# Half-product pairs that begin one pair later and leave one ordinary pair between them, with other banks before them and another order at the end

## The chip, the cores and the metric

The kernel runs on one core of one Trainium2 chip. The metric is the device time of one execution in microseconds (us). Five engines work side by side and wait for each other through semaphores: TensorE (PE) multiplies matrices, VectorE (DVE), ScalarE (ACT) and GpSimd (POOL) work on elements, and SyncE (SP) issues most of the DMAs. Results of PE stand in banks of PSUM; DVE and ACT read them there and so set the bank free for a later matmul.

## The reference

One decoder layer on 512 tokens of width 1024 in float32. A token-mixing part (two causal mixers, their projections, a residual) takes the first two thirds of the time and is not touched here. The channel-mixing part follows:

```python
h = rms_norm(x, norm_ffn_pre[l])
u = causal_dwconv(h @ ffn_up[l], ffn_conv_w[l], ffn_conv_b[l])
u_gate, u_val = jnp.split(u, 2, axis=-1)
x = x + rms_norm((jax.nn.silu(u_gate) * u_val) @ ffn_down[l], norm_ffn_post[l])
```

`ffn_up` has 2 x 2816 columns, that is 44 blocks of 128, or 22 pairs of a gate block and a value block; the convolution has width 3 along the tokens.

## The kernel before, in words

**Numbers in two parts.** Every operand of a matmul is split into a high part (a copy by ACT in a rounded format, L134 or L1698) and a low part (what the rounding lost, a subtraction on DVE or POOL, L172 or L1699). A product is made of three matmuls: high by high, high by low, low by high. So each weight tile of 128x512 costs one DMA, one copy on ACT (the "high", a tile name that ends in h) and one subtraction (the "low", a name that ends in l).

**The up projection** goes over pairs j = 0 to 21. Blocks 2j and 2j + 1 are the pair's gate and value. There are three ways to compute a pair:

- *Ordinary pairs*, those before the first half-product pair, run two blocks of 24 matmuls over 512 tokens (`mm3`). Their weights go through `split_w` with tiles of the pool wp: three buffers for highs and lows (WB), four for raw tiles (RAWB). All their lows are on POOL. The result of block b stands in one of the banks pj, px, py, pz in turn (two buffers each). The name is up with the block and the half: up110 and up111 are block 11's two tiles, pu its result.
- *Half-product pairs* (`seven`, the pairs listed in SEVEN) save one product in eight: with sums and differences of weights and of token quarters, seven products of twelve matmuls over 256 tokens take the place of eight. The results g, v and t stand in PSUM as sg, sv and st; t is always in pz, g and v both in pj for odd pairs, and in px and py for even ones. DVE combines them (L1578). The weights are called sw with the pair and a number: 5, 2, 1, 3, 6, 4, 8 in the order in which PE uses them. Of the seven lows five are on POOL, those of 1 and 8 on DVE. The token forms tf0 to tf3, which these products need, are made by DVE and ACT beside the ordinary pairs.
- *Ordinary pairs between them* (`plain`, L1605) run the same matmuls as the first kind, by quarters, with four sw weights.

The sw weights come from a generator (`coming`), and each product calls the next one, so that five are always ahead. `form_w` deals them out to two rings of buffers by their running number: three of eight go to wp, where the ordinary pairs have theirs as well, five of eight to a ring of their own, sw.

**Eviction of a block.** ACT scales it with the middle tap of the convolution (L1643), DVE adds the two other taps (L1644, L1645), and only then is the bank free. Then come SiLU on ACT (L1653 or L1657) and the product of gate and value (L1654 for ordinary pairs, on POOL, and on DVE for the last two; L1659 for the others), a difference for pairs under 11 (L1661), and the high and the low of the result (L1662, L1667) for the down projection.

**Beside it** POOL issues DMAs that add up weights in DRAM, first for half-product pairs (fs), then for the down projection (ds). The generator `ws` issues one of them at fixed places: one or two for a pair.

**The down projection** uses the same trick: seven products dn of a 2x2 split, each over eleven weight tiles dw and two token tiles. `down_w` takes them in the order of a running number n, loads them and splits them; the low is on POOL when n % 3 is 1. The last product (m = 6) stops four weights short, and these four, the tail (n = 73 to 76), are run token tile by token tile. The sums of the products for the token tiles 2 and 3 are complete when product 5 ends. `post` then does the last step for a token tile: the sum of squares (ACT, L1394), a product with the norm's gain (tm, L1397), the inverse root (ACT, then a reciprocal on DVE, L191), two scalings with the residual added (L1401) and a store of each half. It is called for tiles 2 and 3, and, after the tail's matmuls, for tiles 0 and 1.

**What sets the order.** Each engine runs its instructions in the order of its own queue. A scheduler makes these orders from the program's order and its own estimates; `keep` and `late` hold an instruction to the program's order. Where two engines need a tile they wait for each other by semaphores.

Of the kernel before, what the change touches and what calls it, by code (L numbers as in the profile page):

```python
# [10 lines left out]
F32 = mybir.dt.float32  # L11
F32R = mybir.dt.float32r
AF = mybir.ActivationFunctionType
OP = mybir.AluOpType
# [5 lines left out]
D = 1024  # L20
# [5 lines left out]
V_GMIX, V_GFFN, V_MU, V_MUL, V_W0, V_A0, V_KK, V_KA, V_RK, V_LNW, V_LNB = 0, 8, 16, 40, 43, 51, 59, 67, 75, 83, 91  # L26
WB = 3
RAWB = 4
SEVEN = (6, 7, 8, 9, 10, 11, 12, 14, 15, 16, 18, 19, 20, 21)
SGRP = 2  # L30
UPOS = {j: i for i, j in enumerate(SEVEN + tuple(sorted(set(range(22)) - set(SEVEN))))}
RB = 4
KH, TL = 11, 4
# [19 lines left out]
def hybrid_layer(ctx: ExitStack, tc: tile.TileContext, a, out, dbg=None, stop=None):  # L53
    nc = tc.nc
    te, ve, sc, po, sy = nc.tensor, nc.vector, nc.scalar, nc.gpsimd, nc.sync
# [9 lines left out]
    wp = pool("wp", c=ctx)  # L65
# [43 lines left out]
    junk = xp.tile([128, 1], F32, name="junk")  # L109
# [78 lines left out]
    def rstd_of(ss, n, name, p):  # L188
        st = p.tile([128, 2], F32, tag=name[:2] + "st", name=name, bufs=4)
        act(st[:, 0:1], ss, AF.Sqrt, bias=eps6, scale=1.0 / n)  # L190
        ve.reciprocal(st[:, 1:2], st[:, 0:1])  # L191
        return st[:, 1:2]
# [208 lines left out]
    p2 = lp[2]  # L401
# [572 lines left out]
    for g in range(2):  # L974
        group_tiles(g)
        for i in range(GP):
            p = GP * g + i
# [414 lines left out]
    def post(acc, res, ss, gb, name, p, t, each, x2):  # L1392
        junk = p.tile([128, 512], F32, tag=name + "jk", name=f"{name}jl{t}", bufs=1)
        sc.activation(junk, acc, AF.Square, accum_out=ss[:, 1:2])  # L1394
        tm = p.tile([128, 512], F32, tag=name + "tm", name=f"{name}tm{t}", bufs=2)
        ve.tensor_tensor(ss[:, 2:3], ss[:, 0:1], ss[:, 1:2], op=OP.add)
        ve.tensor_tensor(tm, acc, gb[:, 512:], op=OP.mult)  # L1397
        r = rstd_of(ss[:, 2:3], D, f"{name}r{t}", p)
        for i, q in enumerate((res[:, t, :], tm)):
            hs = slice(i * 512, i * 512 + 512)  # L1400
            ve.scalar_tensor_tensor(x2[t][:, hs], q, r, x2[t][:, hs], op0=OP.mult, op1=OP.add)  # L1401
            each(t, hs)

    op = pool("op", "left", octx)
    x2 = op.tile([128, 4, D], F32, name="x2")
# [74 lines left out]
    with pool("ff") as ff:  # L1480
# [55 lines left out]
        keep = tc.keep_in_program_order  # L1536
        ring = itertools.count()

        def form_w(src, name, eng):
            n = next(ring)  # L1540
            p_, tags, b = (wp, ("raw", "whi", "wlo"), (RAWB, WB)) if n % 8 % 3 == 1 else (sw, ("sraw", "shi", "slo"), (4, 5))
            hi = p_.tile([128, 512], F32R, tag=tags[1], name=name + "h", bufs=b[1])
            lo = p_.tile([128, 512], F32R, tag=tags[2], name=name + "l", bufs=b[1])
            split_to(src, hi, lo, name, 512, eng, p_, late=n < 5, tag=tags[0], bufs=b[0])
            return hi, lo
# [71 lines left out]
        for j in range(22):  # L1617
            us = []
            sv_ = None
            if j == 2:  # L1620
                sw = pool("sw", "right", sctx2)
            if j == SEVEN[0]:
                for _ in side:
                    pass
            if j >= SEVEN[0]:
                sv_ = (seven if j in SEVEN else plain)(j)
            for x in range(2):
                blk = 2 * j + x
                if blk < NU:
                    p = pu4[blk]  # L1630
                    half_up(blk, 1)
                elif sv_ is not None:
                    p = sv_[x]
                else:
                    wh, wl = after.get(blk) or split_w(upw(blk), f"up{blk}")
                    p = ((pj, px, py, pz)[blk % 4] if j < SEVEN[0] else pj)(f"pu{blk}")
                    mm3(p, wslice(wh), wslice(wl), lambda k: h2h[:, k, :], lambda k: h2l[:, k, :])
                if blk == 2 * SEVEN[0] - 1:
                    for _ in range(5):
                        next(coming)  # L1640
                cv = blk * 4
                u = fu.tile([128, S], F32, tag=f"u{x}", name=f"u{blk}", bufs=2)
                sc.activation(u, p, AF.Identity, scale=cvec[:, cv + 2:cv + 3], bias=cvec[:, cv + 3:cv + 4])  # L1643
                ve.scalar_tensor_tensor(u[:, 1:], p[:, :S - 1], cvec[:, cv + 1:cv + 2], u[:, 1:], op0=OP.mult, op1=OP.add)  # L1644
                ve.scalar_tensor_tensor(u[:, 2:], p[:, :S - 2], cvec[:, cv:cv + 1], u[:, 2:], op0=OP.mult, op1=OP.add)  # L1645
                us.append(u)
                if j < SEVEN[0]:
                    for _ in range(1):
                        next(side, None)
                if (j > 2 or x == 0 if j < SEVEN[0] else x == 0 or j not in SEVEN):  # L1650
                    next(ws, None)
            if sv_ is None:
                sc.activation(us[0], us[0], AF.Silu)  # L1653
                (ve if j > SEVEN[0] - 3 else po).tensor_tensor(us[1], us[0], us[1], op=OP.mult)  # L1654
                y = us[1]
            else:
                sc.activation(sv_[0], us[0], AF.Silu)  # L1657
                y = sv_[1] if j >= KH else us[1]
                ve.tensor_tensor(y, us[1], sv_[0], op=OP.mult)  # L1659
            if j < KH:  # L1660
                ve.tensor_tensor(y[:, rgt], y[:, rgt], y[:, lft], op=OP.subtract)  # L1661
            high = sc.activation(ah[:, j, :], y, AF.Copy)  # L1662
            if j == 20:
                last[high.ins.engine] = high
            if j < KH:
                tc.keep_in_program_order(sc.dma_start(t1d[j], y[:, rgt]))
            ve.tensor_tensor(al[:, j, :], y, ah[:, j, :].bitcast(F32), op=OP.subtract)  # L1667
            if j >= KH:
                if j == KH:
                    t2ctx = ExitStack()  # L1670
                    t2 = pool("t2", "left", t2ctx)
                    t1s = [t1_load(0), t1_load(1)]
                else:
                    sy.dma_start(t24d[j - 1 - KH], t24)
                t24 = t2.tile([128, S], F32, tag="t24", name=f"t24{j}", bufs=2)
                ve.tensor_tensor(t24[:, lft], y[:, rgt], t1s[j - KH], op=OP.subtract)
                if j < 20:
                    t1s.append(t1_load(j - KH + 2))
                ve.tensor_tensor(t24[:, rgt], y[:, lft], t24[:, lft], op=OP.subtract)
            if j == 1:  # L1680
                f4ctx.close()
# [3 lines left out]
        def down_w(f, k):  # L1685
            n = next(ring)
            src = a["down4"][f[0], f[1], k] if isinstance(f, tuple) else dsum[k // 2][f][k % 2]
            if n < WB:
                hi, lo = (wp.tile([128, 512], F32R, tag=t, name=f"dw{t}{n}", bufs=WB) for t in ("whi", "wlo"))
            else:  # L1690
                hi, lo = (y[:, (n - WB) % 8, :] for y in (h2h, h2l))
            if n < 8 or n > 9 and n % 8 < 2 or n % 8 >= 6:
                raw = wp.tile([128, 512], F32, tag="raw", name=f"dw{n}r", bufs=RAWB)
            elif n < 10:
                raw = sw.tile([128, 512], F32, tag="sraw", name=f"dw{n}r", bufs=4)
            else:
                raw = ep.tile([128, 512], F32, tag="draw", name=f"dw{n}r", bufs=4)
            load, high = sy.dma_start(raw, src), sc.activation(hi, raw, AF.Copy)  # L1698
            low = (po if n % 3 == 1 else ve).tensor_tensor(lo, raw, hi.bitcast(F32), op=OP.subtract)  # L1699
            if WB <= n < 10:  # L1700
                behind(high)
            if n >= 10:
                keep(load)
                keep(high)
                keep(low)
            return hi, lo
# [5 lines left out]
        with pool("ep") as ep:  # L1712
            res2 = ep.tile([128, 4, 512], F32, name="res2")
            pa, u4 = ([ep.tile([128, 512], F32, name=f"{n}{i}") for i in range(2)] for n in ("pa", "uf"))
            t24 = ep.tile([128, KH, S], F32, name="t24")
            g3 = ep.tile([128, D], F32, name="gb4")
            ep.tile([128, 512], F32, tag="p2jk", name="p2jk", bufs=1)
            s2, x2 = {}, {}

            def store(t, hs):  # L1720
                sy.dma_start(out[t * 128:(t + 1) * 128, hs], x2[t][:, hs])
# [76 lines left out]
            def add(o, x, y, op=OP.add):  # L1798
                return ve.tensor_tensor(o, x, y, op=op)
# [33 lines left out]
            p2 = down(1, (0, 1), 1, 0, py, copies(p1))  # L1833
            p5 = down(2, 0, 0, 1, pz, first_half(p2))
            p4 = down(3, 3, 1, 1, pj, squares(p2), 0)
            p = down(4, 1, 0, 1, px)
            load_x2(0)
            p7 = down(5, 2, 0, 0, py, second_half(p, p5, p4))
            p = down(6, (1, 1), 1, 0, px)
            tail = [down_w((1, 1), k) for k in range(KH - TL, KH)]  # L1840
            for i in range(2):
                keep(add(pa[i], p7[i], pa[i]))
                keep(add(p7[i], p7[i], u4[i]))
                post(p7[i], res2, s2[2 + i], g3, "p2", ep, 2 + i, store, x2)
            for i in range(2):
                for k in range(KH - TL, KH):
                    mms(p[i], 1, 0, k, i, tail[k - KH + TL], False, k == KH - 1)
# [104 lines left out]
```

## Time and profile before

| What | Value |
|---|---|
| three runs, median (lowest to highest) | 1149.72 us (1146.75 to 1150.6) |
| the profiled execution | 1141.52 us, span 1139.7 us |
| PE busy | 1108.8 us, 97% of the span |
| DVE, ACT, POOL busy | 760.7, 644.2, 607.4 us |
| PE's longest wait from 770 us to the end | 6.5 us, at 859 us |
| granted TensorE clock, mean | 0.994 |

Times in rows are us from the start of the span. A row of a timeline has the start, the duration, the engine, the line of the kernel, the operation, output<-inputs, shapes, and, in brackets, how long the engine had stood idle before it and what ended that. PE's matmuls overlap, so their cadence is read from the starts. A row of the waits has who waited for whom: the sum, how often, the longest.

### The profile page before, as it was taken

The numbers are of one execution on the slowest core, as the hardware profiler recorded it, in microseconds if no ns is written. First come the engines' busy times: TensorE is split into PE (matmuls) and PEld (weight loads), VectorE is DVE, ScalarE is ACT, GpSimd is POOL, SyncE is SP. The second block draws the span as 40 slices with busy tenths as digits, with TensorE's granted clock in tenths as the row PEclk, the third lists the DMA queues.
The fourth block names the chain that finished last, engine by engine and source line by source line (L and its number), as shares of the span: only waits on it lengthen the run. The fifth ranks groups of instructions, "written<-read, shape, count | busy, mean of one in ns | idle before, by whom it ended". The sixth has DMA issues, their size and how long they took to land.

```text
span 1139.7 us, 21485 instructions
## 1 busy us (share of the span) xinstructions
PE 1108.8 (97%) x7776; PEld 911.7 (80%) x7776; DVE 760.7 (67%) x1443; ACT 644.2 (57%) x1266; POOL 607.4 (53%) x617
## 2 busy tenths in 40 slices
PE   9999999999999999999999999999997999999996
PEld 7888888877888887767667778888887999897885
DVE  4236655735665553697787745754897987887897
ACT  6447763544666334486666653543555665665554
POOL 4346765545766454576555534540567675654431
PEclk9999999999999999999999999999998999999998
DMA  7524568543666896327576546685677788879983
GB/s 273 133 71 123 153 168 223 158 121 88 184 144 173 236 259 206 94 85 183 175 222 170 133 144 197 204 267 162 193 190 200 248 265 235 268 251 327 292 280 117
DMA packets 121676, 217.00 MB, mean 190 GB/s; under 512 B 37601, under 2 KB 43297, under 8 KB 114914
## 3 DMA queue, kind: packets, MB, share of 16 engines
q1 hardware_dynamic: 95986, 147.07, 40.9%
q0 software_dynamic: 8144, 52.70, 19.7%
q10 hardware_dynamic: 17440, 15.86, 4.4%
q8 instruction: 61, 1.00, 0.3%
q14 instruction: 45, 0.37, 0.1%
HBM read 186.81 MB, written 77.99 MB: 232 GB/s over the span
## 4 chain that ended last, share of the span: by engine, by line
PE 79%; DVE 9%; DMA 5%; ACT 3%; issue 2%; POOL 2%; SPq 0%; ACTq 0%; DVEq 0%; POOLq 0%
PE sg L1573 4%; PE st L1573 4%; PE gt L349 3%; PE ub L1277 3%; PE gt L351 3%; PE gt L350 3%; PE pt L150 3%; PE o L1219 2%; PE ub L1279 2%; PE ub L1278 2%; PE v L349 2%; PE v L350 2%; PE v L351 2%; PE dn L1779 2%; PE dn L1780 2%
## 5 line engine op out<-in xcount | busy, mean ns | idle before, releaser
L1167 ACT ACTIVATE p<-p,stt 128x384 f32<-128x384 f32 (+3 forms) x128 | 70.6, 554 | 31.1 <-DVE stt L1165 30.5
L1165 DVE CUSTOM_DVE_ANT_0 p<-s,rh 128x384 f32<-128x384 f32 (+3 forms) x128 | 59.2, 484 | 20.2 <-PE s L1151 17.1
L1139 POOL TENSOR_SCALAR p<-p,stt 128x512 f32<-128x512 f32 (+1 forms) x64 | 38.8, 613 | 40.8 <-DVE stt L1132 26.3
L1780 PE MATMUL dn<-hh,al 128*128 128x512 f32 x148 | 57.6, 389 | 0.0
L1779 PE MATMUL dn<-hl,ah 128*128 128x512 f32 x148 | 57.6, 389 | 0.0
L1778 PE MATMUL dn<-hh,ah 128*128 128x512 f32 x148 | 57.1, 389 | 0.0
L150 PE MATMUL pt<-ident,p 128*128 128x128 f32 x320 | 44.5, 273 | 1.3 <-DVE p L1141 1.2
L1158 PE MATMUL s<-kst,qs 128*128 128x512 f32 (+1 forms) x128 | 39.1, 395 | 5.8 <-DVE stt L1165 5.6
L150 PEld LDWEIGHTS pt<-ident,p 128*128 128x128 f32 x320 | 37.8, 141 | 7.0 <-DVE p L1141 1.6
L1219 PE MATMUL o<-PT,vt 128*64 128x384 f32 (+3 forms) x256 | 41.0, 443 | 0.0
L1210 ACT ACTIVATE PT<-pt 128x512 f32<-128x512 f32 x48 | 27.4, 586 | 11.9 <-PE pt L150 10.2
L1158 PEld LDWEIGHTS s<-kst,qs 128*128 128x128 f32 x128 | 21.1, 189 | 15.2 <-DVE stt L1165 11.8
L1141 DVE TENSOR_SCALAR p<-p,stt 128x512 f32<-128x512 f32 (+1 forms) x64 | 32.5, 533 | 0.7
L1779 PEld LDWEIGHTS dn<-hl,ah 128*128 128x128 f32 x148 | 27.8, 188 | 5.9
L1778 PEld LDWEIGHTS dn<-hh,ah 128*128 128x128 f32 x148 | 27.8, 188 | 5.7
L1780 PEld LDWEIGHTS dn<-hh,al 128*128 128x128 f32 x148 | 27.8, 188 | 5.7
L1219 PEld LDWEIGHTS o<-PT,vt 128*64 128x64 f32 x256 | 16.3, 136 | 18.3 <-issue 16.0
L251 POOL DMA_DIRECT2D fs<-in_up_dram x42 | 30.5, 733 | 0.4 <-issue 0.4
L1212 DVE COPY PT<-pt 128x512 f32<-128x512 f32 x32 | 21.8, 683 | 9.6 <-PE pt L150 8.5
L273 POOL DMA_DIRECT2D ds<-in_down_dram x36 | 25.2, 774 | 3.2 <-DMA ds<-in_down_dram 3.2
L869 ACT ACTIVATE UV<-xs 64x256 f32<-64x256 f32 x16 | 6.0, 378 | 35.7 <-PE xs L862 35.3
L1167 ACT ACTIVATION_READ_ACCUMULATOR p<-p,stt 128x1 f32 x128 | 24.2, 189 | 0.0
(2301 smaller groups left out, 4265.7 us busy)
## 6 DMA issues: line engine op xcount, KB each, us to landing
fs<-in_up_dram POOLq DMA_DIRECT2D x42, 512.0 KB, 5.9
ds<-in_down_dram POOLq DMA_DIRECT2D x30, 512.0 KB, 7.0
fs<-fs POOLq DMA_DIRECT2D x14, 512.0 KB, 4.6
ds<-ds POOLq DMA_DIRECT2D x10, 512.0 KB, 4.8
gtd<-gt ACTq DMA_DIRECT2D x16, 256.0 KB, 3.6
qs<-qd SPq DMA_DIRECT2D x32, 128.0 KB, 4.3
g<-gtd SPq DMA_DIRECT2D x16, 256.0 KB, 3.6
t24d<-t SPq DMA_DIRECT2D x10, 256.0 KB, 5.2
```

Source lines behind the costliest of these rows:

```text
L150: return te.transpose(o, i, ident)
L349: te.matmul(p, wh(k), hh[:, k, :], start=k == 0, stop=False)
L350: te.matmul(p, wh(k), hl[:, k, :], start=False, stop=False)
L351: te.matmul(p, wl(k), hh[:, k, :], start=False, stop=k == KT - 1)
L1158: m = te.matmul(s_[:, :n], qt, kt[:, x, b, :n], start=x == 0, stop=x == 1)
L1165: ve.tensor_tensor_reduce(sb, parts[b], rh[e][:, (3 - qb) * 128:], -1.0, BIG, OP.add, OP.min, st[e][:, 0, i:i + 1])
L1167: sc.activation(sb, sb, AF.Exp, scale=-1.0, bias=st[e][:, 0, i:i + 1], accum_out=st[e][:, 1, i:i + 1])
L1219: te.matmul(acc[e * 64:e * 64 + 64, j * 128:], vt[:, j, b * 256 + g * 64:b * 256 + g * 64 + 64], m[e][:, c:c + n], start=False, stop=k == ...
L1573: te.matmul(p, w[y][:, ks], x[z][:, k, :], start=first and k + n == 0, stop=last and k == hf - 1 and n == 2, skip_group_check=True)
L1778: te.matmul(p, xh, w[0], start=first, stop=False)
L1779: te.matmul(p, xh, w[1], start=False, stop=False)
L1780: te.matmul(p, xl, w[0], start=False, stop=last)
```

## The change

SEVEN goes from (6 to 12, 14 to 16, 18 to 21) to (7 to 13, 15 to 21). There are fourteen half-product pairs as before. Pair 6 becomes an ordinary one, 13 and 17 become half-product pairs, 14 becomes the one ordinary pair between them. Pair 6, the last ordinary pair, has both blocks in pj. The first five sw weights are asked for in two steps, three after block 12 and two after block 13, where all five came after block 11, and the numbers of `form_w` that go to wp are 3, 5 and 7 of eight instead of 1, 4 and 7, so that the first three are not in wp. The DVE product L1654 follows the count: it is on DVE for pairs 5 and 6 instead of 4 and 5. In the down projection all lows from n = 66 on are on DVE. At the end, `post` is cut in two for tiles 2 and 3: the square and tm first, then, for tile 2, the four tail weights, then the rest.

```diff
-SEVEN = (6, 7, 8, 9, 10, 11, 12, 14, 15, 16, 18, 19, 20, 21)
+SEVEN = (7, 8, 9, 10, 11, 12, 13, 15, 16, 17, 18, 19, 20, 21)
...
-            p_, tags, b = (wp, ("raw", "whi", "wlo"), (RAWB, WB)) if n % 8 % 3 == 1 else (sw, ("sraw", "shi", "slo"), (4, 5))
+            p_, tags, b = (wp, ("raw", "whi", "wlo"), (RAWB, WB)) if n % 8 in (3, 5, 7) else (sw, ("sraw", "shi", "slo"), (4, 5))
...
-                    p = ((pj, px, py, pz)[blk % 4] if j < SEVEN[0] else pj)(f"pu{blk}")
+                    p = ((pj, px, py, pz)[blk % 4] if j < SEVEN[0] - 1 else pj)(f"pu{blk}")
                     mm3(p, wslice(wh), wslice(wl), lambda k: h2h[:, k, :], lambda k: h2l[:, k, :])
-                if blk == 2 * SEVEN[0] - 1:
-                    for _ in range(5):
+                if 2 * SEVEN[0] - 2 <= blk < 2 * SEVEN[0]:
+                    for _ in range(3 - blk % 2):
                         next(coming)
...
-            low = (po if n % 3 == 1 else ve).tensor_tensor(lo, raw, hi.bitcast(F32), op=OP.subtract)
+            low = (po if n % 3 == 1 and n < 6 * KH else ve).tensor_tensor(lo, raw, hi.bitcast(F32), op=OP.subtract)
...
-            tail = [down_w((1, 1), k) for k in range(KH - TL, KH)]
+            def post_a(acc, ss, t):
+                junk = ep.tile([128, 512], F32, tag="p2jk", name=f"p2jl{t}", bufs=1)
+                keep(sc.activation(junk, acc, AF.Square, accum_out=ss[:, 1:2]))
+                tm = ep.tile([128, 512], F32, tag="p2tm", name=f"p2tm{t}", bufs=2)
+                keep(ve.tensor_tensor(tm, acc, g3[:, 512:], op=OP.mult))
+                return tm
+
+            def post_b(tm, ss, t):
+                keep(add(ss[:, 2:3], ss[:, 0:1], ss[:, 1:2]))
+                r = rstd_of(ss[:, 2:3], D, f"p2r{t}", ep)
+                for i, q in enumerate((res2[:, t, :], tm)):
+                    hs = slice(i * 512, i * 512 + 512)
+                    ve.scalar_tensor_tensor(x2[t][:, hs], q, r, x2[t][:, hs], op0=OP.mult, op1=OP.add)
+                    store(t, hs)
+
             for i in range(2):
                 keep(add(pa[i], p7[i], pa[i]))
                 keep(add(p7[i], p7[i], u4[i]))
-                post(p7[i], res2, s2[2 + i], g3, "p2", ep, 2 + i, store, x2)
+                tm = post_a(p7[i], s2[2 + i], 2 + i)
+                if i == 0:
+                    tail = [down_w((1, 1), k) for k in range(KH - TL, KH)]
+                post_b(tm, s2[2 + i], 2 + i)
```

Below are three places in the queues. The first is ACT's queue around the eviction of the last ordinary pair; pu_9515 and pu_9558 are blocks 10 and 11. Before:

```order
L1643 ACTIVATE u_9540<-pu_9515,cvec 128x512
L134 ACTIVATE sw62h<-sw62r 128x512
L134 ACTIVATE sw61h<-sw61r 128x512
L134 ACTIVATE sw63h<-sw63r 128x512
L134 ACTIVATE sw66h<-sw66r 128x512
L1653 ACTIVATE u_9540<-u_9540 128x512
L134 ACTIVATE sw64h<-sw64r 128x512
L134 ACTIVATE sw68h<-sw68r 128x512
L134 ACTIVATE sw75h<-sw75r 128x512
L1643 ACTIVATE u_9613<-pu_9558,cvec 128x512
```

The same queue around the last ordinary pair now; pu_9606 and pu_9666 are blocks 12 and 13:

```order
L1643 ACTIVATE u_9649<-pu_9606,cvec 128x512
L134 ACTIVATE sw76h<-sw76r 128x512
L134 ACTIVATE sw78h<-sw78r 128x512
L134 ACTIVATE sw74h<-sw74r 128x512
L1653 ACTIVATE u_9649<-u_9649 128x512
L134 ACTIVATE sw85h<-sw85r 128x512
L1643 ACTIVATE u_9703<-pu_9666,cvec 128x512
```

Between the two evictions stand four weight highs where there were seven, and the last of them, sw85h, belongs to pair 8.

The second place is POOL's queue at the same stage, as a difference; pair 4's product L1654, which is on POOL now, stands two rows above this piece in the queue now.

```order
 L273 DMA ds_161<-in_down_dram 64x2048
-L172 TENSOR_TENSOR sw64l<-sw64r,sw64h 128x512
+L172 TENSOR_TENSOR up12l_9595<-up120r,up12h_9594 128x512
+L172 TENSOR_TENSOR up12l_9601<-up121r,up12h_9600 128x512
 L172 TENSOR_TENSOR sw75l<-sw75r,sw75h 128x512
 L172 TENSOR_TENSOR sw72l<-sw72r,sw72h 128x512
+L273 DMA ds_165<-in_down_dram 32x2048
+L172 TENSOR_TENSOR up13l_9655<-up130r,up13h_9654 128x512
+L172 TENSOR_TENSOR up13l_9661<-up131r,up13h_9660 128x512
 L172 TENSOR_TENSOR sw73l<-sw73r,sw73h 128x512
```

Pair 6's four lows came in, the two of block 13 behind two lows of pair 7 and a DMA issue.

The third place is DVE's queue near the end, as a difference; dn_12596 is the bank of token tile 2, p2tm the tile tm, p2ss the sums of squares.

```order
+L1799 TENSOR_TENSOR pa_12016<-dn_12596,pa_12016 128x512
+L1799 TENSOR_TENSOR dn_12596<-dn_12596,uf_12018 128x512
+L1844 TENSOR_TENSOR p2tm_12801<-dn_12596,gb_12021 128x512
+L1699 TENSOR_TENSOR hl<-dw73r,hh 128x512
 L1699 TENSOR_TENSOR hl<-dw74r,hh 128x512
 L1699 TENSOR_TENSOR hl<-dw75r,hh 128x512
-L1799 TENSOR_TENSOR pa_12016<-dn_12596,pa_12016 128x512
-L1799 TENSOR_TENSOR dn_12596<-dn_12596,uf_12018 128x512
-L1396 TENSOR_TENSOR p2ss_12694<-p2ss_12694 128x1
-L1397 TENSOR_TENSOR p2tm_12817<-dn_12596,gb_12021 128x512
+L1699 TENSOR_TENSOR hl<-dw76r,hh 128x512
+L1799 TENSOR_TENSOR p2ss_12694<-p2ss_12694 128x1
```

Tile 2's two adds and its tm went ahead of the tail's lows, which are all DVE's now, and its sum of squares behind them.

## Prediction

> **What bounds the kernel now.** I read the page first, then the waits of TensorE (PE) from 770 us to the end, then the chain and the timelines around the longest of them. The page's share of busy time:
>
> ```profile
> span 1139.7 us, 21485 instructions
> PE 1108.8 (97%) x7776; PEld 911.7 (80%) x7776; DVE 760.7 (67%) x1443; ACT 644.2 (57%) x1266; POOL 607.4 (53%) x617
> ```
>
> PE is busy for 97% of the span, so a change that leaves its matmuls alone can win only where PE stands still, or after its last matmul. The change touches nothing before the channel-mixing part, so I ask for PE's waits there (waited for, total, times, longest):
>
> ```profile
> PE st L1573 <- DVE u L1645: 6.5, 1, 6.5
> PE st L1573 <- DVE sv L1578: 1.3, 1, 1.3
> ```
>
> One wait stands out: a product of pair 6, the first half-product pair, waits for the eviction (L1643 to L1645) of the last ordinary block, 11. PE's timeline there, and the chain behind this wait and behind the second one (start, us, what):
>
> ```profile
> 854.84 0.28 PE L1573 MATMUL sg<-hh,sw65h 128*128 128x256 f32 x1
> ...
> 865.74 0.55 PE L1573 MATMUL st<-tf2h,sw63h 128*128 128x256 f32 x1 [6.54 <-DVE u L1645]
> ```
>
> ```profile
> 865.74 2.90 PE st L1573 x12
> 868.64 3.29 PE sg L1573 x24
> 871.93 1.36 PE st L1573 x12
> ...
> 972.35 1.69 PE st L1573 x12
> 974.04 5.49 PE sg L1605 x24
> ```
>
> Twelve matmuls of 256 columns, one product, take 1.36 us; 24 of 512 columns, a block, take 5.49. Behind the long wait the same work is slow: 2.90 instead of 1.36, and 3.29 for two products instead of 2.72. Why the eviction was late shows in the queues of ScalarE (ACT), VectorE (DVE) and GpSimd (POOL):
>
> ```profile
> 853.78 0.62 ACT L134 ACTIVATE sw62h<-sw62r 128x512 fp32r<-128x512 f32 x1
> ...
> 857.95 0.76 ACT L1643 ACTIVATE u<-pu,cvec 128x512 f32<-128x512 f32 x1
> ```
>
> ```profile
> 859.41 5.52 DVE L172 TENSOR_TENSOR sw68l<-sw68r,sw68h 128x512 fp32r<-128x512 f32 x1
> 864.86 0.73 DVE L1645 SCALAR_TENSOR_TENSOR u<-pu,cvec,u 128x510 f32<-128x510 f32 x1
> ...
> 961.89 3.56 DVE L172 TENSOR_TENSOR sw168l<-sw168r,sw168h 128x512 fp32r<-128x512 f32 x1 [0.34 <-ACT sw168h L134]
> ```
>
> ```profile
> 859.24 1.50 POOL L172 TENSOR_TENSOR sw64l<-sw64r,sw64h 128x512 fp32r<-128x512 f32 x1
> ...
> 862.92 1.46 POOL L172 TENSOR_TENSOR sw73l<-sw73r,sw73h 128x512 fp32r<-128x512 f32 x1
> ```
>
> Block 11 ended at about 855, but its L1643 stood behind the weight highs that begin at 853.78, and started at 857.95. Then L1645 stood behind one weight low, sw68l, of 5.52 us; undisturbed such a low takes 0.68 (dw72r, below). It ended just after GpSimd had run four lows back to back, the first at 859.24, the last ending at 864.38.
>
> **The change part by part.** *Matmuls.* None is added or taken; an ordinary pair and one by quarters (L1605) are both two blocks of 24. Nothing.
>
> *Beginning at pair 7, other banks.* Pair 7 takes g and v from bank pj and t from pz. Blocks 12 and 13 now lie in pj, and pz was last used by block 11, a whole pair earlier. So the first two products need only block 12's eviction, which has block 13's 5.49 us for cover. The 6.54 us go, and with them the slow restart, 2.90 - 1.36 + 3.29 - 2.72 = 2.11. Term: -8.7.
>
> [...]
>
> *What is late next.* Two places, both estimates from rows.
> (a) Pair 6 now needs weights of its own. Their highs stand behind pair 4's L1662 and pair 5's L1653, their lows on GpSimd between others and a DMA issue:
>
> ```profile
> 852.58 0.63 ACT L1662 ACTIVATE ah<-u 128x512 fp32r<-128x512 f32 x1 [4.51 <-DVE u L1661]
> ...
> 855.86 0.62 ACT L1653 ACTIVATE u<-u 128x512 f32<-128x512 f32 x1
> ```
>
> ```profile
> 845.75 0.77 POOL L273 DMA_DIRECT2D ds<-in_down_dram  x1
> ...
> 857.44 1.29 POOL L172 TENSOR_TENSOR sw66l<-sw66r,sw66h 128x512 fp32r<-128x512 f32 x1
> ```
>
> If both stay where they are, sw75h follows L1653 and ends at 857.1. GpSimd then has sw75l, sw72l, a DMA issue and up13l in a row, 3 x 1.29 + 0.77, and up13l ends near 861.7. PE wants it with the third matmul of block 13, at 854.84 + 5.49 + 0.45 = 860.8: 0.9 late. But pair 4's L1654 moves from DVE to GpSimd, where it may leave DVE a gap; then L1662 and all behind it come earlier, by more than that 0.9 if the wait of 4.51 shrinks to half. I take the middle, +0.5.
> (b) The third product of pair 7 needs block 13's eviction. Ahead of its L1643 ScalarE has sw85h, in all 0.6 + 0.8 + two DVE steps of 0.75, 2.9 us, against 2.7 for two products: 0.2 late. DVE has sw78l ahead of that L1644; held as sw68l was, it costs 5.52 - 0.68 = 4.8, not held nothing. GpSimd now has a DMA issue and waits for highs among those lows, so I stay near the low end: +0.9 for (b).
> On SP's queue the loads of pair 7's last weights (sw73, sw74, sw78) and of sw85 now come behind block 13's; pair 6 still has matmuls to run while they land, so I count nothing, and without that cover each would be a wait of (a)'s kind. GpSimd's sums for the down projection keep their 27 steps from pair 0 to 21; one moves from pair 17 up to pair 6, long before it is read: nothing.
> Together +1.4, bounds 0 and 0.9 + 0.2 + 4.8 = 5.9. Below nothing is excluded: what (a) and (b) can do at best is to be on time.
>
> *The wait at pair 16.* 1.3 us, and 1.69 instead of 1.36 behind it, 1.6. It came from sw168l, 3.56 us on DVE. Pair 17 is now a half-product pair, GpSimd's order there is another, and seven such pairs stand in a row (15 to 21) where there were three and four. This collision may go and others come: bounds -1.6 and +1.6 (one more of its kind). I lean to the gain, since pairs 7 to 12 ran six in a row without a PE wait over 0.1 us: -0.8.
>
> *The last lows and the end.* PE's last matmul, and DVE to its end:
>
> ```profile
> 1129.72 0.39 PE L1780 MATMUL dn<-hh,al 128*128 128x512 f32 x1
> ```
>
> ```profile
> 1113.13 0.69 DVE L1699 TENSOR_TENSOR hl<-dw66r,hh 128x512 fp32r<-128x512 f32 x1 [1.33 <-ACT hh L1698]
> ...
> 1118.87 0.68 DVE L1699 TENSOR_TENSOR hl<-dw72r,hh 128x512 fp32r<-128x512 f32 x1
> 1119.47 0.68 DVE L1699 TENSOR_TENSOR hl<-dw74r,hh 128x512 fp32r<-128x512 f32 x1
> ...
> 1126.95 0.68 DVE L1799 TENSOR_TENSOR pa<-dn,pa 128x512 f32<-128x512 f32 x1
> ...
> 1135.89 0.74 DVE L1401 SCALAR_TENSOR_TENSOR x2b<-p2tm,p2r,x2b 128x512 f32<-128x512 f32 x1
> ```
>
> DVE sets the end: it works until 1136.63, 6.5 us past PE. From 1113.13 to 1119.47 it did five lows, those of 66, 68, 69, 71 and 72. Without GpSimd a low takes 0.6 from start to start, so all seven (66 to 72) would be done by 1117.4. Then come two adds, ScalarE's square, tm, four lows and the scaling of tile 2; at 0.6 to 0.7 each, with 0.8 for the square and 0.9 from the last low to the first scaling, tile 3's first add comes at 1124.7, 2.3 us earlier than 1126.95. Tile 3 gives most of it back. Its tm now stands ahead of the sum of squares, so the square root is bare (0.5), and the first add on PE's last banks comes behind both scalings (1.3) instead of ahead of them. What is left at the last scaling is about -0.7; bounds -2.3, and +0.5 if the lows don't get faster. PE wants the first tail weight 5.49 us before its end, at 1124.6; its low is done by 1121, so nothing waits there.
>
> The sum: -8.7 + 1.4 - 0.8 - 0.7 = -8.8. The profiled execution took 1141.52 us (the span of 1139.7 and 1.8 around it), so 1132.7 by its own time. The runs shown have a median of 1149.72, 8.2 above it; I carry the difference over: 1140.9.
>
> **Rivals.**
> *The wait comes back at the same place (0.15).* Block 13's eviction meets a held sw78l, and (a) is late in full: +5.9 instead of +1.4, net -4.3, 1145.4. For it: three engines come close there, with margins under 1 us. Against: DVE has one low less in front of that eviction, and no longer pair 4's product.
>
> [...]
>
> *Nothing is late (0.17).* The new waits are 0, pair 16's goes whole, the end gives 1.3: -8.7 - 1.6 - 1.3 = -11.6, 1138.1.
> *The named wait was not what held PE (0.06).* Something else, a weight say, holds pair 7 as long; then pair 16 and the end remain, -1.5: 1148.2. Against it: L1645 ended at 865.59, and PE went on at 865.74.
> *VectorE becomes the bound in pairs 15 to 21 (0.06), slower.* The busy times of two stretches (us, then PE, weight loads, DVE, ACT, POOL), in the run of pairs 7 to 12 and around pair 16:
>
> ```profile
> 880.00:920.00 40.00, 40.00 (x348) 40.00 (x347) 37.22 (x59) 27.54 (x49) 28.77 (x25) 1.00 0.80 253
> 962.00:974.00 12.00, 10.69 (x90) 10.46 (x90) 11.77 (x16) 6.52 (x12) 6.11 (x7) 1.00 0.87 257
> ```
>
> DVE worked for 93% of the first and for 11.77 us in the second, where a pair's seven products take PE 7 x 1.36 = 9.5. If each pair from 15 to 21 took 11.77, that is 7 x 2.27 = 15.9, less the 1.6 that is there already: -8.7 + 1.4 - 0.7 + 14.3 = +6.3, 1156.0. It decides once DVE's work for a pair passes 9.5 us. Against it: the first row gives 8.8 a pair, and PE did not wait in it.
>
> **How the numbers follow.** The forecast has 0.56. A measurement of this kernel can tell about 0.3%, 3.4 us, from no change. Faster: the forecast, "nothing is late" and half of "comes back", 0.81. Same: its other half and "not what held PE", 0.13. Slower: 0.06. The range goes from 1136, which is "nothing is late" with 2 us of scatter of the median, to 1147, "comes back" with as much; the last two rivals stay outside.
>
> **What would show it.** Right: no PE wait of over 2 us between 845 and 875, the products of pair 7 near 1.4 us from the first on; DVE's last scaling about 6 us behind PE's last matmul. Wrong: a wait of several us of pair 7's third product for L1645, or of block 13 for up13l; lows of 3 us and more on DVE in most of the pairs 15 to 21, with PE waiting for L1578; a span that shrinks by less than 4 us.

## The result, and the profile after

The changed kernel takes 1140.65 us (median of 15 runs, 1136.91 to 1145.25); the kernel before, on the same chip, 1146.38 (15 runs). The ratio is 0.9947, 95% interval 0.9933 to 0.996: about 6 us less, between 4.6 and 7.7. The forecast of 1140.9 was met to 0.3 us, but not with the gain that it was built on: it took 8.8 off a median of three runs, 1149.72, and the longer series puts the kernel before 3.3 lower. A gain forecast some 3 us too large met a start some 3 us too high, so the hit to 0.3 us is luck.

The profiled executions show less. Their spans are 1139.7 and 1138.8, 0.9 us apart, and half of what is missing lies ahead of the change. PE's wait for up5l, before anything differs, is over here in the kernel before and in the one after:

```profile
817.04 0.50 PE L234 MATMUL pu<-hh,up5l 128*128 128x512 f32 x1 [0.70 <-POOL up5l L172]
```

```profile
819.47 0.50 PE L234 MATMUL pu<-hh,up5l 128*128 128x512 f32 x1 [0.71 <-POOL up5l L172]
```

In the fourteen profiles of this study that point lies between 817 and 826 us, so spans of single profiles say little, and the prediction's sign of being wrong, a span that shrinks by less than 4 us, came although the runs are 6 us apart. I compare the stretch from there to the end of the span: 1139.7 - 817.04 = 322.7 before, 1138.8 - 819.47 = 319.3 after.

PE's waits after, from 770 us on (who waited for whom: sum, times, longest):

```profile
PE st L1573 <- DVE sv L1578: 3.1, 3, 1.3
PE dn L1779 <- DVE dwwlo L1699: 1.1, 1, 1.1
PE pu L234 <- POOL up5l L172: 0.7, 1, 0.7
PE sv L1573 <- DVE u L1645: 0.5, 1, 0.5
PE pu L234 <- POOL up13l L172: 0.5, 1, 0.5
PE sg L1573 <- DVE u L1645: 0.4, 1, 0.4
...
```

The wait of 6.5 us for L1645 is gone, and two short ones stand in its place. The waits for L1578, inside half-product pairs, have grown from 1.3 to 3.1. PE's timeline has the three waits of the transition and the first of the others:

```profile
863.75 0.50 PE L234 MATMUL pu<-hh,up13l 128*128 128x512 f32 x1 [0.46 <-POOL up13l L172]
...
869.52 0.36 PE L1573 MATMUL sg<-hh,sw75h 128*128 128x256 f32 x1 [0.45 <-DVE u L1645]
...
873.00 0.35 PE L1573 MATMUL sv<-tf0h,sw71h 128*128 128x256 f32 x1 [0.52 <-DVE u L1645]
...
889.88 0.39 PE L1573 MATMUL st<-tf3h,sw88h 128*128 128x256 f32 x1 [1.32 <-DVE sv L1578]
```

What DVE and POOL did there (start, duration):

```profile
862.42 3.07 DVE L1654 TENSOR_TENSOR u<-u,u 128x512 f32<-128x512 f32 x1
...
869.29 1.01 DVE L172 TENSOR_TENSOR sw78l<-sw78r,sw78h 128x512 fp32r<-128x512 f32 x1
...
879.51 3.32 DVE L172 TENSOR_TENSOR sw88l<-sw88r,sw88h 128x512 fp32r<-128x512 f32 x1 [0.16 <-ACT sw88h L134]
```

```profile
861.62 0.76 POOL L273 DMA_DIRECT2D ds<-in_down_dram  x1
862.18 1.52 POOL L172 TENSOR_TENSOR up13l<-up130r,up13h 128x512 fp32r<-128x512 f32 x1
863.43 1.50 POOL L172 TENSOR_TENSOR up13l<-up131r,up13h 128x512 fp32r<-128x512 f32 x1
867.21 1.30 POOL L172 TENSOR_TENSOR sw73l<-sw73r,sw73h 128x512 fp32r<-128x512 f32 x1 [2.28 <-ACT sw73h L134]
...
879.72 1.31 POOL L172 TENSOR_TENSOR sw84l<-sw84r,sw84h 128x512 fp32r<-128x512 f32 x1
880.97 1.30 POOL L172 TENSOR_TENSOR sw95l<-sw95r,sw95h 128x512 fp32r<-128x512 f32 x1
```

DVE is still held at times, but over two GpSimd lows, not four: L1654 beside the two up13l, sw88l beside sw84l and sw95l. L1654 costs the 0.45: behind it come pair 5's high and then L1643 of block 12. The signs that the prediction named as right came: no wait of over 2 us there, products near 1.4 us, and DVE's last scaling 5.8 us behind PE. None of them tells the banks from what follows.

### The profile page after: what moved, and what is told of

It is laid out like the page before. It is cut to its first block, busy times and chain, and to the rows that moved or that the text cites. A ratio compares the mean times of both kernels' runs of the same rounds, so it can differ in the third digit from the quotient of the medians.

```text
span 1138.8 us, 21487 instructions
## 1 busy us (share of the span) xinstructions
PE 1112.4 (98%) x7776; PEld 911.6 (80%) x7776; DVE 753.3 (66%) x1444; ACT 643.0 (56%) x1266; POOL 606.1 (53%) x616
```

## The experiments

Twelve kernels, each timed in turns with the kernel before on one chip. The wait column has PE's waits of over 0.2 us from block 10 to the end of the first half-product pair; the stretch is from the wait for up5l to the end of the span.

| kernel | ratio to before, 95% | waits, us | stretch, us |
|---|---|---|---|
| before | 1 | 6.54 | 322.7 |
| changed | 0.9947 (0.9933 to 0.996) | 0.46 + 0.45 + 0.52 | 319.3 |
| pairs_only | 0.9941 (0.9921 to 0.996) | 0.46 + 0.47 + 0.52 | 318.2 |
| end_only | 0.9991 (0.9973 to 1.0009) | 6.53 | 322.1 |
| banks_only | 0.9974 (0.9957 to 0.9991) | 0.58 + 4.28 | 320.7 |
| old_banks | 0.9932 (0.9916 to 0.9949) | 0.46 | 313.9 |
| low8_gpsimd | 0.9979 (0.996 to 0.9998) | 1.23 + 2.79 | 316.8 |
| banks_low8 | 0.9977 (0.9956 to 0.9998) | 0.72 + 3.29 | 317.8 |
| old_ring | 0.9965 (0.995 to 0.9981) | 0.52 | 318.0 |
| five_at_13 | 0.9936 (0.9913 to 0.9959) | 0.68 | 316.3 |
| burst_off | 0.9914 (0.9887 to 0.9942) | 0.60 + 1.14 | 314.7 |
| three_lows | 0.9969 (0.9951 to 0.9986) | 0.48 + 0.49 + 0.52 | 318.3 |
| combo | 0.993 (0.9906 to 0.9953) | none | 313.6 |
| burst_end | 0.9919 (0.9897 to 0.9941) | 0.59 + 1.13 | 316.6 |

**The two halves of the change.** pairs_only is the changed kernel without the edits of the end, end_only the kernel before with them alone:

```diff
-            low = (po if n % 3 == 1 and n < 6 * KH else ve).tensor_tensor(lo, raw, hi.bitcast(F32), op=OP.subtract)
+            low = (po if n % 3 == 1 else ve).tensor_tensor(lo, raw, hi.bitcast(F32), op=OP.subtract)
...
-                tm = post_a(p7[i], s2[2 + i], 2 + i)
-                if i == 0:
-                    tail = [down_w((1, 1), k) for k in range(KH - TL, KH)]
-                post_b(tm, s2[2 + i], 2 + i)
+                post(p7[i], res2, s2[2 + i], g3, "p2", ep, 2 + i, store, x2)
```

> The changed kernel with the end as it was before (every third low on GpSimd to the last, tile 2's tail weights ahead of its sums, its old order of steps). Theory: the gain sits at the first half-product pair, where the 6.5 us wait and its slow restart are gone; the end gave 0.7 us. So 5 us less than the kernel before (ratio 0.9956), VectorE's last scaling 6.4 to 6.6 us behind the last matmul. Rival: the new order of the end carries as much as the pairs; then it is 3 us less or not even that (0.9975).

> The kernel before with the end alone changed (last lows all on VectorE, tile 2's steps and the tail's lows in the new order). Theory: 0.7 us less, ratio 0.9994, which the times alone can hardly tell from 1; the stretch from the last matmul to the end of the span goes from 9.6 to 8.9 us, and the 6.5 us wait at pair 6 is still there. Rival: the end is worth 2.3 us or more, ratio 0.998.

All of the gain is in the pairs (0.9941), none to be seen in the end (0.9991). And the end's 0.7 us, which the first two profiles show (PE's last matmul to the end of the span: 9.6 before, 8.9 after), can't be put down to the change. The last matmul and what VectorE does last, in pairs_only with the old end:

```profile
1128.67 0.39 PE L1780 MATMUL dn<-hh,al 128*128 128x512 f32 x1
```

```profile
1127.42 0.68 DVE L1799 TENSOR_TENSOR dn<-dn,pa 128x512 f32<-128x512 f32 x1
...
1133.50 0.75 DVE L1401 SCALAR_TENSOR_TENSOR x2b<-p2tm,p2r,x2b 128x512 f32<-128x512 f32 x1
```

and in the changed kernel with the new one:

```profile
1129.56 0.39 PE L1780 MATMUL dn<-hh,al 128*128 128x512 f32 x1
```

```profile
1129.32 0.69 DVE L1799 TENSOR_TENSOR dn<-dn,pa 128x512 f32<-128x512 f32 x1
1130.82 0.16 DVE L1396 TENSOR_TENSOR p2ss<-p2ss 128x1 f32<-128x1 f32 x1 [0.81 <-ACT p2jl L1394]
...
1135.01 0.75 DVE L1401 SCALAR_TENSOR_TENSOR x2b<-p2tm,p2r,x2b 128x512 f32<-128x512 f32 x1
```

DVE ends 5.2 us behind PE with the old end, 5.8 with the new one, where the add for tile 0 waits behind both scalings and its square is bare (0.81). The expected 6.4 to 6.6 was wrong. Last matmul to the end of the span, over six profiles with the old end: 9.6, 8.3, 9.6, 7.8, 8.3, 8.1, mean 8.6; over eight with the new one: 8.9, 8.9, 8.9, 8.1, 8.1, 8.4, 9.0, 9.8, mean 8.8. end_only has the expected 8.9, but that lies inside the scatter of the old end.

**The bank alone.** The kernel before with its last two ordinary blocks in pj, which pair 6 does not use; every engine runs the same instructions in the same order:

```diff
-                    p = ((pj, px, py, pz)[blk % 4] if j < SEVEN[0] else pj)(f"pu{blk}")
+                    p = ((pj, px, py, pz)[blk % 4] if j < SEVEN[0] - 1 else pj)(f"pu{blk}")
```

> The kernel before, where blocks 10 and 11, the last ordinary ones, take their banks from pj, which pair 6 doesn't use; every engine does the same instructions in the same order. Theory that the bank of the late eviction is what holds PE: the 6.5 us wait and the 2.1 us behind it go without any move of the pairs, 8 to 8.7 us less (ratio 0.9925 to 0.993). Rival, that the late queues hold PE whichever bank it is (the weights of pair 6, or the pair's own evictions behind the same queues): the wait comes back at the next product or two, 0 to 3 us less (1.0 to 0.9975).

The rival came true (0.9974, at its edge). PE no longer waits for block 11's eviction, but three products later for pair 6's own sums:

```profile
870.84 0.39 PE L1573 MATMUL st<-tf3h,sw68h 128*128 128x256 f32 x1 [4.28 <-DVE sv L1578]
```

DVE's queue ahead of that sum (the row at 870.35), and POOL's beside it:

```profile
861.77 5.61 DVE L172 TENSOR_TENSOR sw68l<-sw68r,sw68h 128x512 fp32r<-128x512 f32 x1
867.31 0.73 DVE L1645 SCALAR_TENSOR_TENSOR u<-pu,cvec,u 128x510 f32<-128x510 f32 x1
...
870.35 0.43 DVE L1578 TENSOR_TENSOR sv<-st,su 128x256 f32<-128x256 f32 x1
```

```profile
861.60 1.52 POOL L172 TENSOR_TENSOR sw64l<-sw64r,sw64h 128x512 fp32r<-128x512 f32 x1
862.85 1.49 POOL L172 TENSOR_TENSOR sw75l<-sw75r,sw75h 128x512 fp32r<-128x512 f32 x1
864.09 1.50 POOL L172 TENSOR_TENSOR sw72l<-sw72r,sw72h 128x512 fp32r<-128x512 f32 x1
865.35 1.48 POOL L172 TENSOR_TENSOR sw73l<-sw73r,sw73h 128x512 fp32r<-128x512 f32 x1
```

The bank decides who waits first. How long the wait lasts is set by sw68l, which ends at 867.38, 0.6 us after the last of four GpSimd lows in a row. So I changed the theory: the hold on VectorE is the cause, and the next runs test it.

**The old bank in the new place.** The changed kernel with block 13 in pz:

```diff
-                    p = ((pj, px, py, pz)[blk % 4] if j < SEVEN[0] - 1 else pj)(f"pu{blk}")
+                    p = ((pj, px, py, pz)[blk % 4] if j < SEVEN[0] - 1 else (pj, pz)[x])(f"pu{blk}")
```

> The changed kernel with block 13 in pz, so that pair 7's fourth product needs its bank, as pair 6's fourth product needed block 11's before; the order of instructions is that of the changed kernel. Theory that PE stands still only where a late eviction meets a bank wanted early: block 13's eviction ended at 872.9 us here and the fourth product begins at about 873.6, so there is no wait there, the 0.5 us of the third product goes too, and the time is that of the changed kernel less 0.5 (ratio to before 0.994). Rival, that the bank alone was the cause: a wait of 4 us or more of pair 7's fourth product for the eviction, and the time of the kernel before (0.998 to 1.0).

The same conflict costs nothing here, with little to spare. DVE's L1645 of block 13 ends at 878.22, the fourth product (the row of the chain below it) starts at 878.65, right behind the third:

```profile
877.47 0.75 DVE L1645 SCALAR_TENSOR_TENSOR u<-pu,cvec,u 128x510 f32<-128x510 f32 x1
```

```profile
878.65 1.43 PE st L1573 x12
```

So the other banks of the change are not what makes it faster; without them the 0.45 and 0.52 are gone too.

**Who is held.** Next sw68l went to GpSimd, with the old banks (low8_gpsimd) and with those of banks_only (banks_low8):

```diff
-                for x, eng in (((0, 0), po), (2, po), (1, ve), (3, po), ((0, 1), po), (4, po), ((1, 1), ve)):
+                for x, eng in (((0, 0), po), (2, po), (1, ve), (3, po), ((0, 1), po), (4, po), ((1, 1), po if j == SEVEN[0] else ve)):
```

> The kernel before, in which one weight low of pair 6, sw68l, is done by GpSimd instead of VectorE; banks and pairs as before. Theory, after the run with other banks: what costs the time is that VectorE is held in sw68l for 5.5 us while GpSimd runs four lows back to back, and that everything of the last ordinary pair and of pair 6 queues behind it. Then block 11's L1645 follows its L1644 at about 859.4 (times of the kernel before), the fourth product waits 1 us instead of 6.5, and 6 to 7.5 us go, ratio 0.994 to 0.995. Rival: VectorE is held in the next low in its queue, sw71l, ahead of pair 6's sums, and PE waits 3 us or more there; then 1 to 4 us go (0.9965 to 0.999). Rival that the bank alone matters: the wait stays over 5 us, ratio 1.

> The kernel before with both: blocks 10 and 11 in pj, and sw68l on GpSimd. The theory of the held low: no wait over 1 us in pair 6, 8 to 9 us less than before (0.992 to 0.993), which would be the time of the changed kernel or a little under it without the pairs being moved. Rival, the hold moves to sw71l and the sums behind it: a wait of 3 us or more of a product of pair 6 or 7, about 4 us less (0.9965).

The rival again, in kind: the hold moved, though not to sw71l but to the instruction that now met GpSimd's lows, the product L1654. DVE and then PE in banks_low8:

```profile
861.86 4.72 DVE L1654 TENSOR_TENSOR u<-u,u 128x512 f32<-128x512 f32 x1
```

```profile
869.17 0.38 PE L1573 MATMUL st<-tf3h,sw68h 128*128 128x256 f32 x1 [3.29 <-DVE sv L1578]
```

Both gain 2 to 3 us, as banks_only does. Taking away the low that is held helps little as long as the row of lows stays.

**The row broken.** Last, the old pairs with banks_only's banks, and two of GpSimd's lows on VectorE instead of one of VectorE's on GpSimd:

```diff
-                for x, eng in (((0, 0), po), (2, po), (1, ve), (3, po), ((0, 1), po), (4, po), ((1, 1), ve)):
+                for x, eng in (((0, 0), po), (2, po), (1, ve), (3, po), ((0, 1), ve if j == SEVEN[0] else po), (4, ve if j == SEVEN[0] else po), ((1, 1), ve)):
```

> The kernel before with blocks 10 and 11 in pj and two of pair 6's lows, sw66l and sw64l, on VectorE, so that GpSimd has no row of four lows there (it has sw75l, and sw72l and sw73l when their data are there). Theory after the runs so far: VectorE is held in whichever low or product it starts (5.6 us in sw68l, 4.7 us in L1654) until GpSimd's row of lows is over, and pair 6's sums queue behind. Then no instruction of VectorE takes over 3 us between 857 and 872, pair 6's seventh product waits 0 to 1.5 us instead of 4.3, and the kernel is 6 to 8 us below before (ratio 0.993 to 0.995). Rival: VectorE is simply full there, so that two more lows make pair 6's sums later still; a wait of 4 us or more of pair 6, ratio 0.9965 or more.

DVE, which has more to do, is done earlier:

```profile
860.77 1.79 DVE L172 TENSOR_TENSOR sw66l<-sw66r,sw66h 128x512 fp32r<-128x512 f32 x1
862.48 0.68 DVE L172 TENSOR_TENSOR sw64l<-sw64r,sw64h 128x512 fp32r<-128x512 f32 x1
863.09 1.78 DVE L172 TENSOR_TENSOR sw68l<-sw68r,sw68h 128x512 fp32r<-128x512 f32 x1
...
866.34 0.92 DVE L1654 TENSOR_TENSOR u<-u,u 128x512 f32<-128x512 f32 x1
```

```profile
860.25 1.76 POOL L172 TENSOR_TENSOR sw63l<-sw63r,sw63h 128x512 fp32r<-128x512 f32 x1
861.96 0.77 POOL L273 DMA_DIRECT2D ds<-in_down_dram  x1
862.63 1.69 POOL L172 TENSOR_TENSOR sw75l<-sw75r,sw75h 128x512 fp32r<-128x512 f32 x1
865.42 1.29 POOL L172 TENSOR_TENSOR sw72l<-sw72r,sw72h 128x512 fp32r<-128x512 f32 x1 [1.11 <-ACT sw72h L134]
```

Each hold ends with the one GpSimd low that it met, 1.8 us at most. What is left at pair 6 is 0.60 and 1.14, and the ratio is 0.9914, without any move of the pairs. That is about 10 us (6.7 to 13) where 6 to 8 were expected; whether anything beyond the hold adds to it was not traced.

**The feeding edits.** The changed kernel with the old ring of buffers, and with all five weights begun after block 13:

```diff
-            p_, tags, b = (wp, ("raw", "whi", "wlo"), (RAWB, WB)) if n % 8 in (3, 5, 7) else (sw, ("sraw", "shi", "slo"), (4, 5))
+            p_, tags, b = (wp, ("raw", "whi", "wlo"), (RAWB, WB)) if n % 8 % 3 == 1 else (sw, ("sraw", "shi", "slo"), (4, 5))
```

```diff
-                if 2 * SEVEN[0] - 2 <= blk < 2 * SEVEN[0]:
-                    for _ in range(3 - blk % 2):
+                if blk == 2 * SEVEN[0] - 1:
+                    for _ in range(5):
                         next(coming)
```

> The changed kernel with the ring of weight buffers as it was before (places 1, 4 and 7 of eight in the first pool of buffers, not 3, 5 and 7). Theory: the ring only moves single highs and lows by a place or two; the transition to pair 7 and the pairs behind it change by no more than 1 us, ratio to before 0.994 to 0.9955. Rival: the ring's places are what keeps the loads from waiting for a buffer that an ordinary block still uses; then PE waits 2 us or more at block 13 or pair 7, ratio 0.9965 or more.

> The changed kernel with all five of pair 7's first weights begun after block 13, as the kernel before had it at block 11, and not three after block 12 and two after block 13. Theory: block 13's own lows then stand ahead of pair 7's, so its wait of 0.46 us for up13l goes; pair 7's weights come in the 5.4 us of block 13 and the first products; nothing over 1 us, ratio 0.994 to 0.995. Rival: the highs then stand in one row ahead of block 13's L1643 as they did ahead of block 11's, a low on VectorE is held again, and pair 7's second to fourth product waits 3 us or more; ratio 0.9975 or more.

With all five begun after block 13 the whole gain is there (0.9936). With the old ring a gain is left, and whether it is all of it stays open. There the transition waits 0.52 us in all, and pair 13 waits for L1578 instead of pair 8. Its ratio, 0.9965, lies at the edge between the two expectations, and its interval overlaps the changed kernel's: undecided. With five at block 13 the wait for up13l goes and one of 0.68 comes; its rival fell, though the highs stand in one row again: no instruction of VectorE takes over 2.2 us between 855 and 880 us.

**Three lows on VectorE.** The changed kernel with the sixth product's low on VectorE in every half-product pair:

```diff
-                for x, eng in (((0, 0), po), (2, po), (1, ve), (3, po), ((0, 1), po), (4, po), ((1, 1), ve)):
+                for x, eng in (((0, 0), po), (2, po), (1, ve), (3, po), ((0, 1), po), (4, ve), ((1, 1), ve)):
```

> The changed kernel with a third low of every half-product pair on VectorE (that of the sixth product), four left on GpSimd. Theory that the waits at pairs 8, 17 and 18 come from VectorE held beside two GpSimd lows in a row: the lows on VectorE take 1 us on average and seldom 3, the waits for L1578 fall from 3.1 us to under 1, 1 to 2 us less than the changed kernel (ratio to before 0.9925 to 0.994). Rival, VectorE as the bound: it worked 8.8 us a pair of 9.7 already, one low more and its sums behind make it late in most pairs; waits for L1578 of 5 us or more in all, ratio 0.998 or more.

Neither theory holds. The waits for L1578 came to 3.5 us in all, where the changed kernel has 3.1, and moved from pairs 8, 17 and 18 to 11, 12 and 13. The stretches 880 to 940 and 951 to 1020 us, first of the changed kernel, then of three_lows (PE, weight loads, DVE, ACT, POOL):

```profile
880.00:940.00 60.00, 58.68 (x507) 58.48 (x506) 55.46 (x86) 40.70 (x72) 42.66 (x36) 1.00 0.81 246
951.00:1020.00 69.00, 67.19 (x572) 66.55 (x571) 54.34 (x100) 42.88 (x76) 42.74 (x37) 1.00 0.84 261
```

```profile
880.00:940.00 60.00, 58.24 (x497) 57.65 (x496) 55.02 (x87) 37.88 (x68) 32.20 (x27) 1.00 0.77 233
951.00:1020.00 69.00, 68.94 (x575) 68.00 (x574) 59.57 (x110) 45.61 (x80) 36.24 (x32) 1.00 0.90 272
```

In the first stretch POOL does 10 us less and DVE, with more lows, no more than before: what they cost it, it had been held. In the second DVE does 5 us more, and PE is at work for all but 0.06 us. The ratio, 0.9969, lies above the changed kernel's with intervals that overlap: no gain, and no VectorE bound.

**Put together.** combo is the changed kernel with five_at_13 and old_banks, burst_end is burst_off with the new end:

> The changed kernel with pair 7's first five weights begun after block 13 and block 13 in pz, the two variants that did no worse, together. Theory: no PE wait over 0.3 us from block 12 to pair 8, where the changed kernel had 2.75 in four; 1.5 to 3 us less than the changed kernel, ratio to before 0.992 to 0.9935. Rival: what is won at pair 7 comes back as waits of pairs 8 to 21 for L1578, as these fall differently with each shift; the time of the changed kernel, 0.9945 to 0.995.

> The run with two of pair 6's lows on VectorE and blocks 10 and 11 in pj, with the changed kernel's end added: the pairs still begin at 6. Theory, that the end is worth 0.7 us wherever the pairs begin: the stretch from the last matmul to the end of the span is 8.8 to 8.9 us where it was 9.6, the transition's waits of 0.6 and 1.1 us are there again, and the time is 8 to 10.5 us below before (ratio 0.991 to 0.993), at or under that of the changed kernel by 2 to 4 us. Rival: moving the pairs to 7 is worth something by itself, beyond the hold on VectorE; then this kernel is no faster than the changed one, 0.9945 or more.

combo's waits from 840 us to the end:

```profile
PE st L1573 <- DVE sv L1578: 1.4, 3, 0.8
...
```

None is left at the transition; 0.993 is what was expected. Yet GpSimd runs five lows without a gap there, from 862.31 to 869.77. Two of them, and VectorE beside them:

```profile
865.06 1.74 POOL L172 TENSOR_TENSOR sw72l<-sw72r,sw72h 128x512 fp32r<-128x512 f32 x1
866.77 1.74 POOL L172 TENSOR_TENSOR sw73l<-sw73r,sw73h 128x512 fp32r<-128x512 f32 x1
```

```profile
864.65 1.00 DVE L1667 TENSOR_TENSOR al<-u,ah 128x512 fp32r<-128x512 f32 x1 [0.70 <-ACT ah L1662]
865.57 1.78 DVE L172 TENSOR_TENSOR sw71l<-sw71r,sw71h 128x512 fp32r<-128x512 f32 x1
```

VectorE gets in behind each of them: sw71l ends at 867.35, 0.55 us after sw72l, and sw73l takes 1.74 instead of 1.30. So a row of lows by itself does not hold VectorE; the last section says how this row differs from the one of four. burst_end lies where its theory put it too (0.9919), but its stretch from the last matmul to the end is 9.8 us, not 8.9: no gain of the end shows here. By their ratios combo, burst_off and burst_end are the best of the study, 8 to 10 us below the kernel before where the changed one is 6. Their intervals overlap its interval by a little, and they were not timed in turns with it, so that they beat it is likely and not shown.

## Why the prediction was right, and where it was wrong

- **Pair 6's wait and its slow restart, -8.7: right in size, wrong in its cause.** The 6.5 us and the restart are gone, and 2.2 came back at block 13 and pair 7 (next point). But the step gave the credit to the banks and to block 13's cover. banks_only has other banks and keeps most of the wait; old_banks has the old conflict and no wait. The prediction had the right row in hand, sw68l held over four lows, and used it only to explain how late block 11 was. What the change did is put pair 6's own lows and a DMA issue into GpSimd's queue: behind that DMA issue two lows run in a row where four did, and DVE's longest hold in the transition is 3.1 us. burst_off shows that, with banks_only's banks, breaking the row of four is enough; for the changed kernel the same is read from its queues and from the runs that exclude its other edits.
- **Slow restart, 2.11 of it.** It did not come behind every wait. The chains of low8_gpsimd and banks_low8 show the product behind waits of 2.79 and 3.29 us:

```profile
876.15 1.69 PE st L1573 x12
```

```profile
869.17 2.60 PE st L1573 x12
```

  An undisturbed product takes 1.36. The granted clock over these two products is 1.00 and 0.58. Behind 2.79 the matmuls start 0.12 us apart from the second on, behind 3.29 from the fourth on 0.21. The first product behind banks_only's 4.28 takes 2.33, the one behind the 6.54 of the kernel before 2.90 at a clock of 0.50, and the one behind its wait of 1.31 at pair 16 takes 1.69 at 1.00. So the slow restart came behind 3.29, 4.28 and 6.54 and not behind 1.31 and 2.79; what decides in between was not shown.
- **(a) up13l, +0.5: right** (0.46). **(b) the third product, +0.9: near** (0.52); sw78l was not held (1.01). Missed was a third wait of the kind, 0.45 of the first product for block 12's eviction, which I had called covered: L1654, held for 3.07, made it late. Slower products behind the waits add the rest: 2.2 for +1.4, inside the bounds.
- **The wait at pair 16, -0.8: wrong.** Waits for L1578 were 1.3 us before and 3.1 after, at pairs 8, 17 and 18; 1.8 more, above the bound of 1.6. In the other variants that begin at pair 7 with the same lows they are 0.3 (old_banks), 1.4 (combo), 2.0 (five_at_13), 2.1 (old_ring) and 3.1 us (pairs_only), not always at the same pairs. Two of these waits stand behind a held low: pair 16's before (sw168l, 3.56 us) and pair 8's after (sw88l, 3.32). That they all vary with how DVE's work falls beside GpSimd's is an estimate from these two, and a term with a sign could not be had from one profile.
- **The end, -0.7: met in the two profiles and still wrong.** It started from a profile whose end was slow: with the same end the stretch is anywhere from 7.8 to 9.6 us. Over the runs no gain is seen: end_only's interval goes from 3.1 us less to 1.0 more.
- **Not in the sum.** From its first to its last matmul the down projection of the changed kernel took 1.6 us more. Some 1.1 us of it lie between 1078 and 1091 us, where a load of 8.16 us stands in the chain:

```profile
1070.41 8.16 DMA dw43r<-ds
```

  Whether the change shifts that load or the profile scatters was not tried.
- **The rivals.** "The wait comes back" did not happen in the changed kernel, but its mechanism, a held VectorE instruction, is what banks_only, low8_gpsimd and banks_low8 show. VectorE as a bound is out by three_lows. "The named wait was not what held PE" was nearer than its 0.06: banks_only took that wait away and got 3 us of 8.7.

With what the profiles show, the sum would have been -8.7 + 2.2 + 2 + 0 = -4.5 with the L1578 waits of this one profile, just outside the measured -4.6 to -7.7. Not tried were pair 4's L1654 back on VectorE in the changed kernel, and burst_off with the old banks.

## What to carry to other kernels

When a wait ends with an instruction that took eight times its usual time (sw68l, 5.52 us for 0.68), ask first what held that instruction, and look at the neighbour's queue in the same microseconds; moving the waiter, the bank or the held instruction only chose who was late here (waits of 4.28 us in banks_only, 2.79 in low8_gpsimd, 3.29 in banks_low8). Break the neighbour's row instead: spread its work, or give the held engine some of it. Look at the starts, too: the rows that held VectorE longest here (5.61 and 4.72 us) are those in which each low begins about 0.25 us before the last one ends. A term of under 1 us that comes from one profile needs a second profile of the same code before it gets a sign.

## What was not expected of the hardware

VectorE can wait not for one GpSimd instruction but for a row of them: 5.61 us over four lows of 1.5, 4.72 over a row of four that had begun 1.1 us earlier, and 1.8 where a low was followed by a DMA issue. These three (sw68l in banks_only, L1654 in banks_low8, sw66l in burst_off) ended 0.55 to 0.57 us behind the last low that they met, as combo's sw71l ended 0.55 behind sw72l.

Not every row does it. In the row of four each low begins about 0.25 us before the one ahead of it ends; in combo's row it is 0.03. Between 800 and 1025 us of the fourteen profiles, wherever a VectorE instruction with both inputs in SBUF was waiting and GpSimd's next low began 0.22 us or more ahead of the end, it stayed out (30 of 30 places); where the overlap was 0.12 us or less, it got in at 64 of 70. Every row of the first kind begins behind a DMA issue that reads in_down_dram and whose end its first low overlaps, by about 0.2 us, as up13l does above (it begins at 862.18, the issue ends at 862.38); so a DMA issue ends one row and can open a worse one. Why the lows overlap there, and whether moving that issue alone would do, was not tried.

Which instructions are held also shows: lows and L1654, with both inputs in SBUF, stretch (to 5.61 and 4.72 us, where 0.68 is usual); L1644 and L1645, which read a bank, take 0.73 to 0.75 us in all 124 places where one ran beside a GpSimd low between 800 and 1025 us of the profiles before and after.
